# A context Fourier pipeline, shared bias buffers, spread row operations and a fifth begun pair in a two-layer hybrid kernel

## Chip, cores and metric

The kernel runs on one core of a Trainium2 chip. The metric is the device time of one execution in microseconds (us), median of several runs. The engines are named as the profile names them: PE (TensorE, matrix products), DVE (VectorE), ACT (ScalarE), POOL (GpSimd) and SP (SyncE, which issues most loads).

## What is computed

Two layers over 1024 latent tokens and 256 context tokens, width 1024. Layer 0 mixes tokens by a Fourier transform over half of the channels and a two-step long convolution over the other half; layer 1 is a neighbourhood attention with a bias. Each layer ends in a gated FFN, and each mixer and FFN is modulated by six vectors per layer.

```python
for i in range(DEPTH):                       # DEPTH = 2
    sh1, sc1, g1, sh2, sc2, g2 = ada_mod(c, ada_w[i], ada_b[i])      # silu(c) @ w + b, six parts
    u_lat = modulate(rms_norm(h_lat, norm1_g[i]), sh1, sc1)
    ...
    if even: y_lat = mixer_ab(u_lat, *ab); y_ctx = mixer_ab(u_ctx, *ab)
    else:    y_lat, y_ctx = mixer_na(u_lat, u_ctx, w_qkv, w_out, rpb, not last)
    h_lat = h_lat + g1 * y_lat
    h_lat = h_lat + g2 * swiglu(modulate(rms_norm(h_lat, norm2_g[i]), sh2, sc2), gate, up, down)
    ...

def mixer_ab(u, ...):
    p = u @ w_in                              # 1024 -> 2048
    y_f = fourier_mix(p[..., :512])           # 4 groups: real part of fft2 over (tokens, 128 channels)
    y_h = hyena_mix(p[..., 512:], ...)        # short_conv, then v = x1*long_conv(v); v = x2*long_conv(v)
    return concatenate([y_f, y_h]) @ w_out

# attention, per head and chunk of 16 columns: local scores + bias, context scores, one softmax over both
s_loc = q @ k_local * scale + bias;  s_ctx = q @ kc * scale
p = softmax(concatenate([s_loc, s_ctx]));  o = p_loc @ v_local + p_ctx @ vc
```

## The kernel before

All data stand transposed, channels on the 128 partitions, tokens along a row: pieces 0 and 1 are the two halves of the latent tokens (512 each), piece 2 is the context (256). Products are made in three passes, since every operand is split into a high part (cast by ACT, L326) and a low part (difference by DVE, L328): high by high, low by high, high by low. A PSUM tile is `ps` or `pq`, after the pool of banks it comes from. `s`, `t`, `tk`, `g`, `wh`, `wl`, `ws` are SBUF pools with a fixed number of buffers each, taken in turn; a load or a write into a buffer waits until the last reader of that buffer is done. A scheduler sets the order of each engine's instructions from the order in which the program makes them, and each engine runs its own in that order. Generators carry side work: the program calls `next` on one of them between blocks of the main work, and the side work of one step stands behind that block.

The stages that the change touches, with their time in the profiled execution:

- **Input projection** (205 to 470 us), `in_proj`: sixteen blocks of 128 output channels, 24 products on each piece (`lin`). After each block one step of each generator is made: filters of the context (`filt`), one column of the modulation vectors (`ada`, `ada_group`: a column is a 512 KB load and four DVE reductions with their row sum, L507), and from the seventh block on one step of `four`, which is `fourier_c`, the context's Fourier part: for each of four groups it loads the projected rows, folds them (POOL and ACT), multiplies by the channel matrices (`channels`, PE, then splits on ACT and DVE), multiplies by the token matrix (PE) and writes the result (`fourier_out`). One step is one group, with all of this in sequence. `conv` begins the context's convolution in the last two blocks. Modulation groups 2 and 3, eight columns each, are made here, group 4 in the output projection.
- **Convolution** (470 to 680 us): `forward_c` transposes the context's value and multiplies it with class matrices; `turned` (L981) transposes the latent value into eight tiles, each split by ACT and DVE; `unit` makes the two spectra of one frequency block and class, in two halves, and hands them to `combine_l` (L949), which multiplies with the filter on DVE and POOL; `turn_x` (L1006) transposes the gate. Eight units make order 0, then `inverse_first` goes back to tokens for the first gate, and eight more units make order 1: the first halves of four of these are begun in `inverse_first`. Matrices are loaded in float32 and cast by ACT (`cmat`, `cmat2`, L374 and L388), or loaded by POOL's queue with the cast in the transfer (`cast`), into the weight pools.
- **Output projection** (680 to 800 us), `out_proj`: group 0 is pieces 2 and 0, group 1 is piece 1. `fill` gives side work between blocks; here that is modulation group 4. `after1` is called behind each group: it normalises the context, then runs all steps of `wino_first`, the first sums of the FFN's Winograd form, behind group 0.
- **First FFN, context part** (800 to 930 us): `load_cond` (L488) loads the two condition vectors again and applies Silu on ACT.
- **Attention** (1750 to 2215 us), `attn_item`: 64 items (16 heads, two row halves, two pairs of column chunks). An item takes two 192 KB bias tiles from pool `G`, makes local and context scores on PE, adds the bias and takes the row maximum on DVE (L2091, `st` and `g`), exponentials on ACT, transposes on PE (L2108), splits them on ACT and DVE (L2111, L2112), and multiplies with the values.
- **Last FFN's start** (2275 to 2335 us): pairs of products are begun (`wino_begin`) before the normalisation's factor `r1` is known, since the factor can be applied to the product. `wino_second` then makes the sums that need the factor (T1 splits, L1495 on ACT and L1496 on DVE), which the product L1605 waits for.

## Time and profile before

| | |
|---|---|
| median of three runs | 2943.41 us (2942.9 to 2945.5) |
| profiled execution | 2940.22 us |
| its span, first to last instruction | 2938.5 us (1.7 us lie around it) |
| mean granted PE clock | 0.987 |
| PE busy in the span | 2824.0 us, 96% |
| DVE, ACT, POOL busy | 2044.7, 1334.5, 534.0 us |
| sum of PE's idle gaps ahead of products | 106.9 us |

A row of waits reads "engine, line and tile that waited <- engine, tile and line that released it: us in total, times, longest". A row by stretch reads "start:end length, then busy us (and count) of PE, PE's weight loads, DVE, ACT and POOL, then granted clock as a share of full speed, DMA share, GB/s". Busy time and waits overlap between engines; only what PE waits for lengthens a stage in which PE is last.

### The profile page before, as it was taken

How to read it: one execution, taken by the hardware profiler on the slowest of the kernel's cores; microseconds unless marked ns; L12 is line 12 of the kernel's file. 1: busy time of each engine (PE TensorE's matmuls, PEld its weight loads, DVE VectorE, ACT ScalarE, POOL GpSimd, SP SyncE). 2: the span in 40 equal slices, each digit the busy share in tenths (PEclk: the TensorE clock that was granted, in tenths of full speed). 3: DMA queues.
4: the chain of work that ended last, by engine and by line, in shares of the span. 5: the costliest groups of instructions: out<-in, count | busy, mean ns of one | idle time of the engine just before them, and what ended most of it. 6: DMA issues, size and time to landing. Idle time of an engine off the chain costs nothing.

```text
span 2938.5 us, 44126 instructions
## 1 busy us (share of the span) xinstructions
PE 2824.0 (96%) x15704; PEld 2361.3 (80%) x15704; DVE 2044.7 (70%) x3742; ACT 1334.5 (45%) x2282; POOL 534.0 (18%) x860
## 2 busy tenths in 40 slices
PE   8899998899999999999999999999989899999998
PEld 3678787788899888888888888888777688888886
DVE  6775676859776888966777536677668877765555
ACT  4543324543454333333445327777655533333433
POOL 2112112351100211212010002333212022111000
PEclk9999999999999999999999999999999999999999
DMA  9664434566556555659884446777846276434763
GB/s 338 218 214 157 150 103 130 186 220 230 201 175 194 196 199 199 226 183 331 303 309 153 138 130 153 179 194 174 238 144 239 80 243 218 169 110 163 229 194 129
DMA packets 303914, 568.39 MB, mean 193 GB/s; under 512 B 83144, under 2 KB 129930, under 8 KB 303694
## 3 DMA queue, kind: packets, MB, share of 16 engines
q1 hardware_dynamic: 242750, 373.11, 40.9%
q0 software_dynamic: 58640, 188.26, 18.1%
q10 hardware_dynamic: 2304, 4.20, 0.4%
q8 instruction: 124, 2.03, 0.3%
q14 instruction: 96, 0.79, 0.1%
HBM read 415.49 MB, written 119.80 MB: 182 GB/s over the span
## 4 chain that ended last, share of the span: by engine, by line
PE 73%; issue 10%; DMA 8%; DVE 5%; ACT 2%; POOL 1%; SPq 1%; POOLq 0%; DVEq 0%; ACTq 0%
PE ps L1605 24%; PE ps L322 23%; PE pq L322 12%; PE ps L1777 5%; PE pq L1605 3%; PE ps L1889 2%; PE pq L1777 2%; DMA s<-d 1%; DMA g<-in_bias 1%; PE ps L2108 1%; DMA mat<-in_ada_k 1%; DMA s<-in_c_ctx 1%; PE ps L1111 1%; DMA s<-in_x_t 1%; DVE wl L328 1%
## 5 line engine op out<-in xcount | busy, mean ns | idle before, releaser
L1605 PE MATMUL ps<-s,s 128*128 128x512 f32 x2008 | 498.2, 391 | 6.0 <-DVE s L1496 4.7
L1605 PEld LDWEIGHTS ps<-s,s 128*128 128x128 f32 x2008 | 377.4, 188 | 88.0 <-DVE s L1496 6.7
L322 PE MATMUL ps<-s,wh 128*128 128x256 f32 (+1 forms) x1584 | 356.4, 327 | 4.1 <-ACT wh L326 3.9
L322 PE MATMUL pq<-s,wh 128*128 128x512 f32 (+1 forms) x1040 | 319.7, 384 | 6.0 <-ACT s L794 2.1
L322 PEld LDWEIGHTS ps<-s,wh 128*128 128x128 f32 x1584 | 264.1, 191 | 29.9 <-ACT wh L326 5.2
L322 PE MATMUL ps<-s,s 128*128 128x65 f16 (+4 forms) x2780 | 241.2, 240 | 25.9 <-DVE st L2091 12.8
L1777 PE MATMUL ps<-s,s 128*128 128x512 f32 (+1 forms) x1000 | 259.5, 383 | 3.1 <-DVE s L328 3.0
L328 DVE TENSOR_TENSOR wl<-ws,wh 128x1024 fp32r<-128x1024 f32 (+1 forms) x142 | 169.7, 1196 | 127.0 <-ACT wh L326 122.5
L326 ACT CAST s<-s 128x1024 fp32r<-128x1024 f32 (+2 forms) x184 | 168.1, 941 | 190.3 <-DMA s<-d 161.4
L326 ACT CAST wh<-ws 128x1024 fp32r<-128x1024 f32 (+1 forms) x142 | 145.7, 1026 | 233.8 <-PE ps L322 90.2
L322 PE MATMUL ps<-s,wl 128*128 128x256 f32 (+1 forms) x792 | 237.5, 326 | 2.7 <-DVE wl L328 2.7
L322 PEld LDWEIGHTS pq<-s,wh 128*128 128x128 f32 x1040 | 192.2, 192 | 42.6 <-ACT s L794 3.4
L326 ACT CAST s<-t 128x512 fp32r<-128x512 f32 (+1 forms) x213 | 121.9, 587 | 220.2 <-PE ps L1605 81.9
L328 DVE TENSOR_TENSOR s<-s,s 128x1024 fp32r<-128x1024 f32 (+2 forms) x162 | 185.6, 1177 | 49.1 <-ACT s L326 46.6
L1777 PEld LDWEIGHTS ps<-s,s 128*128 128x128 f32 x1000 | 184.6, 188 | 40.9 <-DVE s L328 4.4
L322 PE MATMUL pq<-s,wl 128*128 128x512 f32 (+1 forms) x520 | 197.5, 381 | 1.5 <-DVE wl L328 1.5
L322 PE MATMUL ps<-s,mat 128*128 128x512 f32 x714 | 180.5, 403 | 18.6 <-ACT s L326 11.0
L328 DVE TENSOR_TENSOR s<-t,s 128x512 fp32r<-128x512 f32 (+1 forms) x213 | 138.1, 658 | 77.6 <-ACT s L326 49.4
L1605 PE MATMUL ps<-s,wh 128*128 128x512 f32 x608 | 189.0, 390 | 0.0
L322 PEld LDWEIGHTS ps<-s,mat 128*128 128x128 f32 x714 | 135.8, 193 | 55.3 <-ACT s L326 13.7
L322 PEld LDWEIGHTS ps<-s,wl 128*128 128x128 f32 x792 | 148.0, 190 | 15.9 <-DVE wl L328 3.5
L322 PEld LDWEIGHTS ps<-s,s 128*128 128x128 f32 (+1 forms) x860 | 132.7, 194 | 31.2 <-ACT s L326 9.9
(436 smaller groups left out, 5532.9 us busy)
## 6 DMA issues: line engine op xcount, KB each, us to landing
s<-d SPq DMA_DIRECT2D x283, 256.0 KB, 4.0
s<-in_down SPq DMA_DIRECT2D x150, 256.0 KB, 3.9
d<-s POOLq DMA_DIRECT2D x137, 256.0 KB, 3.1
s<-in_ada_w POOLq DMA_DIRECT2D x64, 512.0 KB, 5.1
d<-tk POOLq DMA_DIRECT2D x98, 256.0 KB, 3.5
g<-in_bias SPq DMA_DIRECT2D x128, 192.0 KB, 2.8
ws<-in_up SPq DMA_DIRECT2D x44, 512.0 KB, 4.0
d<-g POOLq DMA_DIRECT2D x87, 256.0 KB, 3.0
```

What stands on the lines that cost most here:

```text
L322: self.nc.tensor.matmul(o, l, r, start=st, stop=sp)
L326: self.last_hi = nc.scalar.copy(hi, src).ins
L328: self.last_lo = eng.tensor_tensor(lo, src, hi.bitcast(F32), SUB).ins
L1111: nc.tensor.matmul(d, s, w, start=cb not in first, stop=e == 1 and i == 1 and f == 3 and k == 2, skip_group_check=True)
L1605: nc.tensor.matmul(ps, x[:, sl], y, start=first and j == 0 and x is wh and y is xh, stop=j == 3 and x is wl, skip_group_check=True)
L1777: m = nc.tensor.matmul(acc[j][:, c0:c1], x[:, sl], y[:, xs], start=first and k == 0, stop=last and k == 2, skip_group_check=True)
L1889: m = nc.tensor.matmul(o, x[:, nb * P:(nb + 1) * P], t[:, c:c + 256], start=kb == 0 and k == 0 and nb % 2 == 0, stop=kb == NFB - 1 and k = ...
L2108: nc.tensor.transpose(ps[:, j * P:(j + 1) * P], src[:, j * P:(j + 1) * P], self.ident)
```

## The change

Seven edits. `fourier_c` becomes a pipeline of seven steps, begun one block earlier: in one step the output of group k−3, the token product of group k−2, the channel products of group k−1 and the fold of group k. Modulation group 4 moves from the output projection into the input projection, where two columns are made a step for eleven steps. The class matrices of the context are loaded by the casting queue, its class steps move from the projection's end into the first two units, and PE's gate transposes follow the last value transpose. Two of the second convolution's units get matrices by the casting queue in `S4` buffers (`cast4`), and the eighth takes banks of the other pool. `wino_first` becomes side work of the output projection's group 1, whose weights are fetched two ahead; the reload of the conditions ahead of that projection goes. `load_cond` moves from after the first FFN's context blocks into their last stage. Every second attention item (`c0` not 0) takes one 768-wide tile from the weight pool `ws` and one load instead of two. Before the last FFN a fifth half, (2, 0), is begun.

The diff, cut to its core:

```diff
@@ -398,2 +398,8 @@
 
+    def cast4(self, src):
+
+        m = self.S4(F32R)
+        self.ldr(m, src)
+        return m
+
     def lin(self, wh, wl, off, ks, x, pcs, view=lambda x: x):
@@ -841,6 +847,6 @@
                     next(g, None)
-            if i > 5:
+            if i > 4:
                 next(four, None)
-            if i > 13:
-                next(conv, None)
+            if i == 14:
+                next(conv)
             if nb < 4:
@@ -895,2 +901,6 @@
         PS = self.PS if o == 0 else self.PQ
+        if o == 0:
+            ms = [self.S2(F32R), self.S2(F32R)]
+            for i in range(4):
+                self.ldr(ms[i // 2][:, i % 2 * 256:i % 2 * 256 + 256], a["vf_c"][i, 0])
         for j in (0, 1):
@@ -907,3 +917,3 @@
                 xh, xl = tr[(i + i // 2) % 2]
-                mt = self.cmat(256, a["vf_c"][i, 0], small=o == 0)
+                mt = ms[i // 2][:, i % 2 * 256:i % 2 * 256 + 256] if o == 0 else self.cmat(256, a["vf_c"][i, 0])
                 ps = PS()
@@ -980,3 +990,4 @@
             for cb in range(4):
-                nc.tensor.transpose(ps[:, cb * P:(cb + 1) * P], self.ab["l"][cb][:, j * P:(j + 1) * P], self.ident)
+                last = nc.tensor.transpose(ps[:, cb * P:(cb + 1) * P], self.ab["l"][cb][:, j * P:(j + 1) * P], self.ident)
+            self.after_turned = last.ins
             hi, lo = self.S2(F32R), self.S2(F32R)
@@ -1005,3 +1016,4 @@
             x = (self.xrev if rev else self.xrow)[cb][:, j * P:j * P + P]
-            self.nc.tensor.transpose(ps[:, cb * P:(cb + 1) * P], x, self.ident)
+            with self.follow(self.after_turned):
+                self.nc.tensor.transpose(ps[:, cb * P:(cb + 1) * P], x, self.ident)
         t = self.S2()
@@ -1010,3 +1022,3 @@
 
-    def unit(self, o, fb, cls, bank=None):
+    def unit(self, o, fb, cls, bank=None, wide=False):
 
@@ -1016,3 +1028,3 @@
             src = a["vfe_l"][fb]
-            mt = self.cast(1024, src) if o + fb == 0 else self.cmat(1024, src)
+            mt = self.cast4(src) if wide else self.cast(1024, src) if o + fb == 0 else self.cmat(1024, src)
             mats = [mt[:, :512], mt[:, 512:]]
@@ -1022,3 +1034,4 @@
             src = a["vfo_l"][fb]
-            mats = [self.cast(1024, src[:, j * 1024:j * 1024 + 1024]) for j in (0, 1)] if o + fb == 0 else self.cmat2(src)
+            half = [src[:, j * 1024:j * 1024 + 1024] for j in (0, 1)]
+            mats = [self.cast4(x) for x in half] if wide else [self.cast(1024, x) for x in half] if o + fb == 0 else self.cmat2(src)
             xs = [range(4, 8), range(4)]
@@ -1371,20 +1384,27 @@
             mats[i] = m
-        raws = []
-        for g in range(4):
-            p0, p1 = self.S2(F32, 128), self.S2(F32, 128)
-            self.ld(p0, self.pd[g][:, 0:128])
-            self.ld(p1, self.pd[g][:, 128:256])
-            prs = self.folded(p0, p1, P, q[:, g:g + 1], qn[:, g:g + 1], nc.gpsimd)
...
-            raw = self.S2()
-            self.fourier_out(ps[:, 0:128], ps[:, 128:256], raw, P, self.T)
-            raws.append(raw)
+        raws, prs, opd, got = [], {}, {}, {}
+        for k in range(7):
+            if k >= 3:
+                raw = self.S2(F32, 256)
+                ps = got.pop(k - 3)
+                self.fourier_out(ps[:, 0:128], ps[:, 128:256], raw, P, self.T)
+                raws.append(raw)
+            if 0 <= k - 2 < 4:
+                ae, ao, am = opd.pop(k - 2)
+                ps = got[k - 2] = self.PS()
+                for i, (xh, xl) in enumerate((ae, am, ao)):
+                    m = mats[i]
+                    self.mm(ps[:, :256], xh, m[:, :256], i == 0, False)
+                    self.mm(ps[:, :256], xl, m[:, :256], False, False)
+                    self.mm(ps[:, :256], xh, m[:, 256:], False, i == 2)
+            if 0 <= k - 1 < 4:
+                opd[k - 1] = self.channels(prs.pop(k - 1), cg, 1, self.PS)
+            if k < 4:
+                p0, p1 = self.S2(F32, 128), self.S2(F32, 128)
+                self.ld(p0, self.pd[k][:, 0:128])
+                self.ld(p1, self.pd[k][:, 128:256])
+                prs[k] = self.folded(p0, p1, P, q[:, k:k + 1], qn[:, k:k + 1], nc.gpsimd)
             yield
         self.middle(cgf, q, qn, mid, self.PS)
+        yield
         for g in range(4):
@@ -1416,2 +1436,3 @@
         fetch()
+        fetch()
         for g, pcs in enumerate(groups):
@@ -1444,4 +1465,2 @@
                                 evict(nb, pc, accs[(nb, pc)])
-                    if k:
-                        next(fill, None)
             for nb in range(0 if g else 4, KB):
@@ -1452,5 +1471,5 @@
                     evict(nb, pc, acc[pc])
-                if g == 0:
-                    next(fill, None)
-                    next(fill, None)
+                if g:
+                    with self.follow(self.last_lo):
+                        next(fill, None)
             after(pcs)
@@ -1690,3 +1709,2 @@
                 last = lo
-            self.load_cond()
             todo = (x for l1, m in [(0, 5)] + [(1, m) for m in range(6)]
@@ -1747,2 +1765,4 @@
                     sums(k)
+            if i == 0 and u is not None:
+                self.load_cond()
             for _ in range(3 if i < 8 else 2):
@@ -2066,9 +2086,14 @@
         rlo = 4 * hf
-        bias, loc = [], []
+        loc = []
         pctx = self.PS()
+        if c0:
+            t = self.W("ws", "bias", F32, 768)
+            self.ld(t.rearrange("p (i k) -> p i k", i=2), a["bias"][head, hf, c0:c0 + 2].rearrange("i p k -> p i k"))
+            bias = [t[:, :384], t[:, 384:]]
+        else:
+            bias = [self.G(F32, 384), self.G(F32, 384)]
+            for i in (0, 1):
+                self.ld(bias[i], a["bias"][head, hf, c0 + i])
         for i in (0, 1):
             c = c0 + i
-            b = self.G(F32, 384)
-            self.ld(b, a["bias"][head, hf, c])
-            bias.append(b)
             q = [t[:, c * P:(c + 1) * P] for t in qs]
@@ -2270,3 +2295,3 @@
         self.load_cond()
-        ada = (x for m in (2, 3) for x in self.ada_group(0, m, (0, 1), "s2"))
+        ada = (x for m in (2, 3, 4) for x in self.ada_group(0, m, (0, 1), "s2"))
         filt = (x for g in (self.filter_raw("c", raws["c"]), self.filter_spectrum("c", 0, raws["c"][0]),
@@ -2290,3 +2315,3 @@
         fc, cc = four(), conv()
-        self.in_proj(u, ((filt, (1,)), (ada, (1,))), fc, cc)
+        self.in_proj(u, ((filt, (1,)), (ada, (2,) * 11 + (1, 1, 1, 0))), fc, cc)
         drain(ada)
@@ -2297,3 +2322,2 @@
         self.banks = 6
-        next(cc, None)
         self.xt, self.sums_due = {}, None
@@ -2307,6 +2331,6 @@
             self.turn_x(k)
-            if k == 6:
+            if k in (0, 1, 6):
                 next(cc)
         self.parts()
-        units = [self.unit(1, fb, cls, self.PQ if k == 3 else None)
+        units = [self.unit(1, fb, cls, self.PQ if k % 4 == 3 else None, k in (2, 3))
                  for k, (fb, cls) in enumerate(((0, 1), (1, 1), (2, 1), (0, 0), (1, 0), (3, 1), (2, 0), (3, 0)))]
@@ -2355,10 +2379,14 @@
                 load_h((1,))
-                for _ in self.wino_first(h, 0, 3, rs[1]):
-                    pass
+                rest.append(rs[1])
             else:
+                drain(first)
                 rest.append(self.rms((1,))[0])
 
+        def first_row():
+            yield from self.wino_first(h, 0, 3, rest.pop())
+
+        first = first_row()
+
         load_h((2, 0))
-        self.load_cond()
-        self.out_proj("w_out", y, [(2, 0), (1,)], h, 0, 2, after1, self.ada_group(0, 4, (0, 1), "s4"))
+        self.out_proj("w_out", y, [(2, 0), (1,)], h, 0, 2, after1, first)
         for b in range(8):
@@ -2493,2 +2521,3 @@
         begun[(1, 1)] = self.wino_begin(1, 1, 1, self.TK, self.S2)
+        begun[(2, 0)] = self.wino_begin(1, 2, 0, self.G, self.S2)
         self.ffn(1, None, h4, hs1, self.wino_second(h2, 1, 3, r1), after4, begun=begun)
```

Where instructions now stand. First PE at the end of the input projection; `pq` and `ps` are the last block's sums, `s_..` the operands, `g` the gate's rows. Before:

```order
L322 MATMUL ps_1128_4377<-s2_1106_4248,s2_1127_4374 128x512
L322 MATMUL ps_1128_4377<-s2_1107_4249,s2_1127_4374 128x512
L322 MATMUL ps_1128_4377<-s2_1106_4248,s2_1127_4374 128x512
L322 MATMUL ps_1131_4385<-s2_1109_4257,s2_1130_4382 128x512
L322 MATMUL ps_1131_4385<-s2_1110_4258,s2_1130_4382 128x512
L322 MATMUL ps_1131_4385<-s2_1109_4257,s2_1130_4382 128x512
L1006 MATMUL pq_1199_4594<-c_1_86,g_1193_4580 128x128
L1006 MATMUL pq_1199_4594<-c_1_86,g_1195_4584 128x128
```

After:

```order
L322 MATMUL ps_1174_4423<-s4_502_1610,wl_1172_4418 128x512
L322 MATMUL ps_1175_4424<-s4_503_1611,wl_1172_4418 128x512
L991 MATMUL ps_1179_4514<-c_1_86,s4_1097_3909 128x128
L991 MATMUL ps_1179_4514<-c_1_86,s4_1118_4036 128x128
L991 MATMUL ps_1179_4514<-c_1_86,s4_1137_4160 128x128
L991 MATMUL ps_1179_4514<-c_1_86,s4_1150_4283 128x128
L991 MATMUL ps_1182_4523<-c_1_86,s4_1097_3909 128x128
```

Before, the context's class products (two groups of three) and the gate's transposes (L1006) follow the last block, and the value's transposes (L981) come later; now the value's transposes (L991) follow at once, all eight tiles of them, and the gate's transposes come behind these.

Second PE at the last FFN's start. L1605 before and L1624 after are products of the FFN; those on `wh` and `wl` are begun pairs, those on two `s` tiles are the first product that needs the T1 splits. Before:

```order
L1605 MATMUL ps_5083_24195<-s2_5005_23847,wh_5079_24175 128x512
L1605 MATMUL ps_5083_24195<-s2_5004_23846,wl_5080_24176 128x512
L1605 MATMUL ps_5368_24452<-s4_5330_24338,s2_5024_23926 128x512 x2
L1605 MATMUL ps_5368_24452<-s4_5330_24338,s2_5025_23927 128x512
L1605 MATMUL ps_5368_24452<-s4_5331_24343,s2_5024_23926 128x512 x2
L1605 MATMUL ps_5368_24452<-s4_5331_24343,s2_5025_23927 128x512
L1605 MATMUL ps_5368_24452<-s4_5332_24348,s2_5024_23926 128x512 x2
L1605 MATMUL ps_5368_24452<-s4_5332_24348,s2_5025_23927 128x512
```

After:

```order
L1624 MATMUL ps_5053_24143<-s4_4937_23641,wh_5051_24138 128x512 x2
L1624 MATMUL ps_5055_24158<-s4_4940_23657,wh_5051_24138 128x512 x2
L1624 MATMUL ps_5340_24415<-s4_5302_24301,s2_4990_23854 128x512 x2
L1624 MATMUL ps_5340_24415<-s4_5302_24301,s2_4991_23855 128x512
L1624 MATMUL ps_5340_24415<-s4_5303_24306,s2_4990_23854 128x512 x2
L1624 MATMUL ps_5340_24415<-s4_5303_24306,s2_4991_23855 128x512
L1624 MATMUL ps_5340_24415<-s4_5304_24311,s2_4990_23854 128x512
L1624 MATMUL ps_5053_24143<-s4_4937_23641,wl_5052_24139 128x512
L1624 MATMUL ps_5053_24143<-s4_4946_23679,wh_5051_24138 128x512 x2
L1624 MATMUL ps_5053_24143<-s4_4946_23679,wl_5052_24139 128x512
```

Before, the T1 product follows the last begun pair; now it starts inside a begun pair, the fifth, (2, 0) (`ps_5053`, `ps_5055`), whose remaining products stand between the third and the fourth T1 operand.

Third ACT at the end of the first FFN's context part. L488 before and L494 after are Silu on the reloaded conditions, L326 casts of weights. Before:

```order
L1684 ACTIVATE t_2330_9070<-ps_2328_9020 128x256
L488 ACTIVATE s4_2366_9288<-s4_2366_9288 128x512 x2
L326 CAST wh_2348_9155<-s4_2347_9154 128x1024
L1684 ACTIVATE t_2341_9140<-ps_2339_9090 128x256
L326 CAST wh_2356_9219<-s4_2355_9218 128x1024
L1684 ACTIVATE t_2352_9210<-ps_2350_9160 128x256
L488 ACTIVATE s4_2367_9293<-s4_2367_9293 128x512 x2
L326 CAST wh_2359_9225<-s4_2358_9224 128x1024
```

After:

```order
L1703 ACTIVATE t_2328_9062<-ps_2326_9012 128x256
L494 ACTIVATE s4_2417_9540<-s4_2417_9540 128x512
L326 CAST wh_2346_9147<-s4_2345_9146 128x1024
L1703 ACTIVATE t_2339_9132<-ps_2337_9082 128x256
L494 ACTIVATE s4_2417_9540<-s4_2417_9540 128x512
L494 ACTIVATE s4_2418_9545<-s4_2418_9545 128x512
L326 CAST wh_2354_9211<-s4_2353_9210 128x1024
L1703 ACTIVATE t_2350_9202<-ps_2348_9152 128x256
L326 CAST wh_2357_9217<-s4_2356_9216 128x1024
L494 ACTIVATE s4_2418_9545<-s4_2418_9545 128x512
```

The call moved in the code, but the four activations still stand among the casts of the same weights; the pairs are apart now.

More of the change, by code (lines that the diff above doesn't have):

```diff
@@ L1371, in fourier_c @@
             mats[i] = m
-        raws = []
-        for g in range(4):
-            p0, p1 = self.S2(F32, 128), self.S2(F32, 128)
-            self.ld(p0, self.pd[g][:, 0:128])
-            self.ld(p1, self.pd[g][:, 128:256])
-            prs = self.folded(p0, p1, P, q[:, g:g + 1], qn[:, g:g + 1], nc.gpsimd)
-            ae, ao, am = self.channels(prs, cg, 1, self.PS)
-            ps = self.PS()
-            for i, (xh, xl) in enumerate((ae, am, ao)):
-                m = mats[i]
-                self.mm(ps[:, :256], xh, m[:, :256], i == 0, False)
-                self.mm(ps[:, :256], xl, m[:, :256], False, False)
-                self.mm(ps[:, :256], xh, m[:, 256:], False, i == 2)
-            raw = self.S2()
-            self.fourier_out(ps[:, 0:128], ps[:, 128:256], raw, P, self.T)
-            raws.append(raw)
+        raws, prs, opd, got = [], {}, {}, {}
[20 more added lines that the diff above has]
+                prs[k] = self.folded(p0, p1, P, q[:, k:k + 1], qn[:, k:k + 1], nc.gpsimd)
             yield
         self.middle(cgf, q, qn, mid, self.PS)
+        yield
         for g in range(4):
```

## The prediction

> **What bounds the kernel now.** I read the page's busy times first, then who waited for whom on TensorE (PE), then busy time and granted clock by stage. Page:
>
> ```profile
> PE 2824.0 (96%) x15704; PEld 2361.3 (80%) x15704; DVE 2044.7 (70%) x3742; ACT 1334.5 (45%) x2282; POOL 534.0 (18%) x860
> ```
>
> PE is busy 2824 us of a span of 2938.5, so it bounds the kernel. The diff takes no matrix product away; a change that only moves work can therefore win PE's idle 114 us, and what slow clock follows that idle time. Who ends the idle time (line waited for: us in total, times, longest):
>
> ```profile
> PE ps L322 <- ACT s L326: 18.1, 12, 5.2
> PE ps L322 <- DVE st L2091: 12.8, 8, 3.1
> PE pq L1006 <- DVE s L816: 6.1, 1, 6.1
> PE ps L1605 <- DVE s L1496: 4.7, 3, 2.9
> PE ps L322 <- DVE s L949: 4.6, 1, 4.6
> ...
> PE ps L322 <- ACT mat L388: 1.7, 1, 1.7
> ```
>
> Where it lies, one stage a row (stretch, its length, busy us of PE, PEld, DVE, ACT, POOL with counts, granted clock, DMA share, GB/s):
>
> ```profile
> 205.00:320.00 115.00, 112.51 (x609) 96.14 (x609) 69.85 (x180) 37.32 (x80) 24.95 (x38) 0.99 0.43 145
> 320.00:400.00 80.00, 72.97 (x390) 61.21 (x389) 49.96 (x163) 25.75 (x60) 4.80 (x5) 0.96 0.38 127
> 400.00:470.00 70.00, 70.00 (x356) 59.29 (x355) 53.07 (x124) 14.90 (x22) 17.12 (x19) 1.00 0.35 113
> 470.00:490.00 20.00, 11.60 (x57) 9.35 (x56) 15.24 (x25) 10.38 (x19) 5.02 (x4) 0.83 0.27 92
> 566.00:615.00 49.00, 38.26 (x157) 30.15 (x155) 33.30 (x39) 19.15 (x21) 17.17 (x11) 0.93 0.66 225
> 680.00:800.00 120.00, 116.59 (x613) 98.95 (x611) 98.38 (x209) 49.62 (x81) 16.77 (x32) 1.00 0.61 223
> 905.00:930.00 25.00, 22.08 (x177) 21.68 (x176) 11.15 (x14) 10.60 (x17) 3.26 (x6) 0.95 0.69 219
> 1780.00:2215.00 435.00, 407.07 (x3829) 355.37 (x3827) 298.23 (x684) 314.40 (x709) 119.08 (x190) 0.98 0.72 184
> 2300.00:2335.00 35.00, 28.98 (x112) 21.30 (x111) 35.00 (x57) 19.11 (x34) 0.00 (x0) 0.90 0.09 30
> 2400.00:2500.00 100.00, 100.00 (x443) 82.81 (x442) 72.75 (x110) 33.58 (x55) 21.67 (x40) 1.00 0.61 213
> ```
>
> The first seven are the input projection (three rows), its end, the second convolution's spectra, the output projection and the end of the first FFN's context part; then attention and the last FFN's start. The last row is the rate without waits: 443 matrix products in 100 us, 0.226 us each. After many waits the clock is halved for a while:
>
> ```profile
> 326.90:330.30 3.40, 3.39 (x14) 3.15 (x15) 1.29 (x5) 1.65 (x6) 0.00 (x0) 0.50 0.02 5
> 477.10:483.90 6.80, 5.38 (x20) 4.73 (x21) 6.11 (x13) 2.03 (x5) 0.59 (x1) 0.50 0.50 174
> 576.10:579.50 3.40, 3.06 (x8) 2.15 (x7) 3.40 (x7) 1.84 (x3) 0.00 (x0) 0.50 1.01 375
> 610.20:613.60 3.40, 3.40 (x10) 2.66 (x9) 3.40 (x4) 0.00 (x0) 2.70 (x2) 0.50 0.13 51
> 2125.70:2129.10 3.40, 3.40 (x15) 2.72 (x12) 2.46 (x7) 1.75 (x5) 0.52 (x1) 0.50 0.82 241
> 2183.70:2190.50 6.80, 5.58 (x42) 5.10 (x42) 5.23 (x12) 2.70 (x7) 0.00 (x0) 0.50 0.12 45
> 2306.60:2313.40 6.80, 4.49 (x9) 2.65 (x10) 6.80 (x12) 3.41 (x6) 0.00 (x0) 0.50 0.00 0
> ```
>
> I count half of PE's busy time in such a stretch as lost: 1.7 us for a short one, 2.7, 2.8 and 2.2 us for the three long ones. These losses go if the wait ahead of them goes.
>
> The wait ahead of the stretch at 2125.7 is no long one:
>
> ```profile
> 2124.84 1.12 PE L322 MATMUL ps<-s,s 128*128 128x65 f16 x30 [2.38 <-DVE st L2091]
> ```
>
> 2.38 us of idle time were enough. The Trainium skill ("TensorE: Matmul & The Clock Gate", section on the HAM clock gate) says that the half clock sets in after at least one idle window of about 3.4 us. By that rule waits shorter than 3.4 us would earn no clock back, and of the credits below the 4.5 us for attention and the 2 for the FFN would fall; here the row differs, so the measurement decides and I keep them.
>
> **The change, part by part.** For each part: the most it can win (idle plus half-clock loss), what it adds, and the value I take.
>
> *A, input projection (205 to 470).* The context's Fourier part ran fold, channel products, group product and output of one group in one step, serially; now each of seven steps holds one stage of up to four different groups, so PE meets operands made a projection block earlier. PE's idle time from 320 to 400 is 80 − 73.0 = 7.0 us; the half-clock stretch at 327 is 1.7. Against it stands modulation group 4 (eight columns), which moves here from the output projection, two columns a step instead of one. What the eight cost there, on DVE alone and in line L507 alone:
>
> ```profile
> 690.00:745.00 55.00, 20.92 (x64) 1.00 0.55 203
> ```
>
> So 21 us of DVE work and eight 512 KB loads on SP join stretches where DVE now works 69.9 + 50.0 = 120 us of 195: on average 141 of 195, still beside PE. But DVE takes instructions in order, and it stands behind those loads (205 to 400):
>
> ```profile
> DVE tk L507 <- DMA s<-in_ada_w: 18.9, 4, 8.4
> ...
> DVE t L507 <- DMA s<-in_ada_w: 4.5, 4, 2.8
> ```
>
> A wait there holds up the low parts of the next weights (L328), which PE needs. Upper end 8.7; lower end by the rival below. I take +2: half of that less some 2 us of new waits.
>
> *B, end of the projection (470 to 490).* Now PE goes from the last block to the context's class products and the gate's transposes (L1006), whose bank is freed by the short convolution's L816 (6.1 us), then to the transposes of the value (L981). Afterwards it goes straight to the eight value transposes, whose inputs are made blocks earlier; the class products move among the first units. Idle 20 − 11.6 = 8.4, clock 2.7: at most 11.1. What remains: eight transposed tiles wait for banks which ACT and DVE free by splitting,
>
> ```profile
> L328 DVE TENSOR_TENSOR s<-t,s 128x512 fp32r<-128x512 f32 (+1 forms) x213 | 138.1, 658 | 77.6 <-ACT s L326 49.4
> ```
> ```profile
> 604.23 1.03 PE L899 MATMUL pq<-c,s 128*128 128x128 f32 x8
> ```
>
> 8 × 0.66 = 5.3 us of splits on DVE beside 32 transposes, four times the second row, 4.1 us: a stall of at least 1.2, and the short convolution's own row operations come first on DVE. I put the stall at 5 in all (as long as the splits) and take +6; bounds 0 to 11.
>
> *C, second convolution (566 to 615).* Two units get matrices by a casting DMA into buffers of their own, so their first halves can stand before PE's wait: 42 instead of 24 products in front of it, 18 × 0.226 = 4.1 us more cover. Who ended PE's idle time in this stretch:
>
> ```profile
> PE ps L322 <- ACT s L326: 4.2, 2, 3.9
> ```
>
> The cover hides that 3.9 us wait and the change drops the ACT cast wait (1.7, L388) and the stretch at 576 (1.5). The fourth unit of each four takes the other bank pool, which is against the 4.6 us wait on L949 and its stretch at 610 (1.7); yet L949 must still come in DVE's order, so I take none of it. +7; bounds 0 and 49 − 38.3 + 3.2 = 13.9.
>
> *D, output projection.* Idle 120 − 116.6 = 3.4 there; the 21 us leave DVE, weights are fetched one further ahead, and the first Winograd sums move from one block after group 0 into the blocks of group 1. +2; bounds −3 (these sums now late) to +3.4.
>
> *E, reload of the conditions.* In the code it moves behind the first block's row; in ACT's order the four activations stay between the casts of the same weights, and these casts wait behind them now:
>
> ```profile
> ACT s L488 <- DMA s<-in_c: 5.8, 2, 4.7
> ...
> ACT s L488 <- DMA s<-in_c_ctx: 4.3, 2, 3.4
> ```
>
> Idle 25 − 22.1 = 2.9 stays: 0, bounds −1 to +2.9.
>
> *F, attention.* Every second item takes its two bias tiles as one 384 KB load into the four-deep weight pool; the others keep both G buffers, so loads can be asked for about four items ahead instead of two. 128 loads become 96. Now:
>
> ```profile
> DVE g L2091 <- DMA g<-in_bias: 19.3, 14, 3.1
> ...
> DVE s L2112 <- ACT s L2111: 41.5, 22, 3.9
> ```
>
> The first row is the wait that should vanish; behind it on DVE stand the row maximum and all that follows, and PE waits for L2091 12.8 us (8 times). The clock lost at 2125.7 and 2183.7 is 1.7 + 2.8 = 4.5. At most 17.3. DVE then waits for ACT as in the second row, so I take not half: +8. Weights share the pool, but a weight load is asked for some 600 products before its use, at 435/3829 us a product about 70 us. Lower end −2.
>
> A page bears on the joining of loads: the Trainium skill ("DMA: Bandwidth & Descriptors", section Bandwidth) advises batches of 1 MiB and more, since each transfer carries a fixed cost. By that rule the joined load alone would earn something; here the present 192 KB loads land in 2.8 us (median), no run shows a joined one, and I count nothing for it.
>
> ```profile
> g<-in_bias SPq DMA_DIRECT2D x128, 192.0 KB, 2.8
> ```
>
> *G, last FFN's start.* A fifth half (24 products, 24 × 0.226 = 5.4 us) is begun ahead, and the normalisation's end stands one begun pair earlier, so the T1 splits (L1496) start up to 5.4 us sooner and have 5.4 more to hide behind, against 4.7 us of waits. Idle 35 − 29 = 6.0 and clock 2.2: at most 8.2. DVE is full in that stretch (35.0 of 35), so the fifth pair's own splits (about 3 us) come off: +5; bounds −1 to 8.2.
>
> **Sum.** 2 + 6 + 7 + 2 + 0 + 8 + 5 = 30 us. The profiled execution took 2940.22 us (span 2938.5 and 1.7 around it): 2910. The runs' median is 2943.4, 3.2 above, so 2913 is my forecast, 1.0% faster.
>
> **The rivals.** (1) *The waits only change names.* In C, F and G the releaser is DVE, and DVE's own queue (L2112 behind ACT, L949, full at 2300) is then the limit; left are A 2, B 6, the 3.9 + 1.5 of C and D 2, less 3 of new DVE waits: 12, so 2931. For it: 41.5 us of DVE waits that no edit touches; against: in attention DVE is busy 298 of 435. Chance 0.20. (2) *Everything acts.* 9 + 11 + 14 + 3 + 0 + 13 + 8 = 58, the upper bounds with attention at three quarters, and I leave 3 of it for new waits: 55, so 2888. Chance 0.10. (3) *An edit does nothing*: the moved condition reload, by the order of ACT. It is in my sum at 0; if it did act, 2.9 less. (4) *Slower: DVE becomes the bound in the input projection.* In order, each step now stands behind two modulation loads. DVE's free time from 205 to 470 is 265 − 173 = 92 us, 71 after the moved work, so 5.9 us for each of the twelve double steps. If the second load comes later than that, each us more costs 12. At the longest wait seen, 8.4, it is 2.5 × 12 = 30 and twelve short half-clock stretches, 20: 50 against the 28 of B to G, 22 slower: 2965. For it: four such waits already, 4.7 us on average; against: that is below 5.9, and the second row of part A has none above 2.8. Chance 0.13. (5) *Halfway to that*, gains and loss cancel, 2943: 0.07.
>
> **How the numbers follow.** Forecast 0.50 (2913, 2898 to 2925), rivals as above. Range 2888 to 2946: from everything acting to a cancelled gain, leaving out rival 4 and a little below. About 0.2% (6 us) is what a measurement can tell from no change: faster 0.50 + 0.20 + 0.10 = 0.80, same 0.07, slower 0.13.
>
> **What would show it.** After: no wait of PE on L816's successor, PE below 3 us idle at 470 to 490; no DVE wait for bias loads, and the PE row for the bias line under 6 us; no wait over 1 us for T1 splits; the casts of two units gone from ACT; the row of modulation waits on DVE under 25 us. I am wrong if PE is idle over 15 us between 205 and 470, or if attention stays near 435 us with DVE waiting for ACT in place of the loads.

## The result, and the profile after

The changed kernel takes 2925.23 us (median of 4 runs, 2923.48 to 2929.05) against 2943.15 before: ratio 0.994, 95% interval 0.9923 to 0.9958, about 18 us less. The forecast was 2913, so direction and range hold and the gain is 18 us where 30 stood in the sum. The profiled span is 2921.6 us against 2938.5. The page's busy times:

```profile
PE 2821.2 (97%) x15704; PEld 2361.3 (81%) x15704; DVE 2045.4 (70%) x3742; ACT 1325.3 (45%) x2271; POOL 533.0 (18%) x859
```

As many products as before; only waiting and slow clock changed. By stretch, cut in both traces at the same products (the last of the projection's blocks, the last value transpose L981 or L991, the inverse's first and last product, the FFN's first, the first and the last attention transpose, the 801st product of the last FFN):

| stretch | before | after | forecast gain | gain |
|---|---|---|---|---|
| input projection (A) | 263.4 | 266.2 | 2 | −2.8 |
| its end, to the last value transpose (B) | 18.5 | 7.7 | 6 | 10.8, or 7.2 without the moved products |
| spectra and units, then the inverse's end (C) | 125.1 + 69.1 | 124.9 + 74.3 | 7 | −5.0, or −1.4 without them |
| output projection to FFN (D, E) | 248.4 | 247.6 | 2 | 0.8 |
| attention (F) | 431.5 | 417.0 | 8 | 14.5 |
| last FFN's start (G) | 257.6 | 258.3 | 5 | −0.7 |

Twelve class products (12 × 0.226 = 2.7 us) and eight gate transposes (8 × 0.11 = 0.9 us) moved from B's stretch to C's. The other stretches lie within 1.1 us. The changed kernel's rows by stretch (the two parts of C are rows 3 and 4; columns as before):

```profile
207.20:473.40 266.20, 255.71 (x1353) 218.77 (x1352) 193.03 (x550) 76.59 (x159) 49.05 (x65) 0.97 0.44 145
473.40:481.10 7.70, 5.37 (x35) 5.16 (x34) 7.12 (x14) 6.82 (x12) 0.00 (x0) 0.78 0.55 175
481.10:606.00 124.90, 114.57 (x525) 92.99 (x523) 94.37 (x123) 61.45 (x81) 54.51 (x45) 0.97 0.59 197
606.00:680.30 74.30, 70.38 (x466) 65.13 (x467) 46.83 (x88) 31.76 (x55) 28.94 (x35) 0.93 0.62 203
1777.80:2194.80 417.00, 400.66 (x3818) 351.96 (x3816) 297.76 (x682) 309.32 (x702) 119.25 (x190) 0.99 0.73 192
2194.80:2453.10 258.30, 248.46 (x1109) 201.14 (x1108) 211.59 (x323) 116.09 (x193) 46.43 (x86) 0.99 0.56 195
```

In attention DVE has no wait for bias loads left (it had 19.3 us), and its wait for ACT's L2136 is a little longer. The list of DVE's waits there begins:

```profile
DVE s L2137 <- ACT s L2136: 47.1, 25, 3.9
DVE st L2158 <- PE ps L322: 17.6, 16, 2.9
```

PE's waits over the whole span (of the changed kernel; L2116 is the bias line, L959 the combination, L515 the row sum of a modulation column, L539 the sum of squares):

```profile
PE ps L322 <- ACT s L326: 9.9, 6, 5.2
PE ps L322 <- DVE s L328: 6.6, 5, 4.0
...
PE ps L322 <- DVE st L2116: 3.8, 4, 1.1
PE pq L322 <- DVE c L515: 3.6, 1, 3.6
PE pq L322 <- DVE s L959: 3.4, 1, 3.4
PE ps L322 <- DVE tk L539: 3.2, 1, 3.2
```

Of the old heads of the list, the wait for L816 is gone and those for T1 splits are smaller; the wait for the combination is not: L949 is L959 now, and 4.6 us have become 3.4 beside further waits of 2.0 and 2.3. The last three rows are one single wait each, and each lies in a stretch that lost.

### The profile page after: what moved, and what is told of

Same layout as the page of the kernel before. It is cut to its first block, busy times and chain, and to the rows that moved or that the text cites. A ratio compares the mean times of both kernels' runs of the same rounds, so it can differ in the third digit from the quotient of the medians.

```text
span 2921.6 us, 44070 instructions
## 1 busy us (share of the span) xinstructions
PE 2821.2 (97%) x15704; PEld 2361.3 (81%) x15704; DVE 2045.4 (70%) x3742; ACT 1325.3 (45%) x2271; POOL 533.0 (18%) x859
## 5 line engine op out<-in xcount | busy, mean ns | idle before, releaser
L1624 PE MATMUL ps<-s,s 128*128 128x512 f32 x1956 | 483.6, 389 | 0.3 <-ACT s L326 0.3
L1624 PEld LDWEIGHTS ps<-s,s 128*128 128x128 f32 x1956 | 367.0, 188 | 77.6 <-ACT s L326 1.1
L322 PE MATMUL ps<-s,wh 128*128 128x256 f32 (+1 forms) x1700 | 386.0, 333 | 8.6 <-DVE s L328 4.6
L322 PEld LDWEIGHTS ps<-s,wh 128*128 128x128 f32 x1700 | 284.8, 193 | 39.7 <-DVE s L328 5.5
L322 PE MATMUL pq<-s,wh 128*128 128x512 f32 (+1 forms) x924 | 278.9, 378 | 3.4 <-DVE s L2429 2.0
L328 DVE TENSOR_TENSOR wl<-ws,wh 128x1024 fp32r<-128x1024 f32 (+1 forms) x141 | 168.7, 1197 | 143.8 <-ACT wh L326 139.3
L326 ACT CAST wh<-ws 128x1024 fp32r<-128x1024 f32 (+1 forms) x141 | 144.7, 1026 | 262.2 <-PE ps L322 129.9
L1797 PE MATMUL ps<-s,s 128*128 128x512 f32 (+1 forms) x1000 | 259.8, 383 | 3.3 <-DVE s L328 3.1
L322 PE MATMUL ps<-s,wl 128*128 128x256 f32 (+1 forms) x850 | 254.5, 331 | 0.5 <-DVE wl L328 0.5
L326 ACT CAST s<-s 128x1024 fp32r<-128x1024 f32 (+2 forms) x184 | 167.8, 940 | 191.2 <-DMA s<-d 166.7
L328 DVE TENSOR_TENSOR s<-s,s 128x1024 fp32r<-128x1024 f32 (+2 forms) x162 | 185.5, 1176 | 56.5 <-ACT s L326 54.0
L1797 PEld LDWEIGHTS ps<-s,s 128*128 128x128 f32 x1000 | 184.4, 188 | 41.7 <-DVE s L328 5.4
L326 ACT CAST s<-t 128x512 fp32r<-128x512 f32 (+1 forms) x208 | 119.9, 590 | 177.6 <-PE ps L1624 73.3
L322 PEld LDWEIGHTS pq<-s,wh 128*128 128x128 f32 x924 | 168.3, 190 | 33.5 <-DVE s L2429 2.4
L1624 PE MATMUL ps<-s,wh 128*128 128x512 f32 x600 | 187.4, 392 | 0.0
L328 DVE TENSOR_TENSOR s<-t,s 128x512 fp32r<-128x512 f32 (+1 forms) x208 | 136.7, 667 | 67.4 <-ACT s L326 44.4
L322 PE MATMUL ps<-s,mat 128*128 128x512 f32 x678 | 171.5, 399 | 11.3 <-ACT s L326 6.9
L322 PE MATMUL pq<-s,wl 128*128 128x512 f32 (+1 forms) x462 | 173.3, 377 | 0.0
L322 PEld LDWEIGHTS ps<-s,wl 128*128 128x128 f32 x850 | 159.1, 192 | 16.5 <-DVE wl L328 0.8
```

Of the source, the lines that this page charges most:

```text
L322: self.nc.tensor.matmul(o, l, r, start=st, stop=sp)
L326: self.last_hi = nc.scalar.copy(hi, src).ins
L328: self.last_lo = eng.tensor_tensor(lo, src, hi.bitcast(F32), SUB).ins
L1624: nc.tensor.matmul(ps, x[:, sl], y, start=first and j == 0 and x is wh and y is xh, stop=j == 3 and x is wl, skip_group_check=True)
L1797: m = nc.tensor.matmul(acc[j][:, c0:c1], x[:, sl], y[:, xs], start=first and k == 0, stop=last and k == 2, skip_group_check=True)
```

## Experiments

The theory after the result: the bias edit carries the whole gain; in the projection the pipeline wins and the second modulation column a step loses; among the units a bank choice loses what the casting queue wins; at the last FFN the fifth half moves idle time. The main rival: the new waits are noise of one trace, or come from something ahead of them.

**Bias edit alone.** The kernel before with only:

```diff
...
+        if c0:
+            t = self.W("ws", "bias", F32, 768)
+            self.ld(t.rearrange("p (i k) -> p i k", i=2), a["bias"][head, hf, c0:c0 + 2]...)
...
```

> The kernel before with the attention bias edit alone. If the 14.6 us that the changed kernel won between the first and the last transpose of attention (431.3 to 416.7 us) are this edit's, attention takes 416 to 419 us here and the kernel is 13 to 16 us faster than before (about 2928 us). If part of that came from what runs ahead of attention (another order of loads, another state of the buffers), attention gains under 8 us.

2926.74 us, ratio 0.9946 (0.9933 to 0.996); attention:

```profile
1777.60:2192.10 414.50, 398.48 (x3818) 348.83 (x3816) 297.55 (x682) 309.08 (x702) 119.36 (x190) 1.00 0.73 193
```

17.0 us less than before, and all other stretches within 3 us of before. In all thirteen kernels here that have this edit attention takes 414.5 to 418.2 us, against 431.5 before. So this edit alone gives what the whole change gives, and all the others together come to about nothing.

**Lead or joined load.** The changed kernel with

```diff
-            self.ld(t.rearrange(...), a["bias"][head, hf, c0:c0 + 2]...)
+            for i in (0, 1):
+                self.ld(bias[i], a["bias"][head, hf, c0 + i])
```

> The changed kernel, each wide bias tile filled by two 192 KB loads instead of one of 384 KB. If the gain is the longer lead of the loads (more buffers), nothing is lost: attention stays at 416 to 418 us and no wait of DVE for bias loads comes back. If the gain is the joined load (fewer transfers), up to half of the 14.6 us is lost: attention at 420 to 425 us.

2921.36 us (ratio 0.993, 0.9918 to 0.9942); attention 417.0 us, to the tenth as with the joined load, and no wait for bias loads. The gain is the lead: buffers, not the number of transfers.

**Group 4 back**, with one column a step, and **serial Fourier part** with two:

```diff
-        ada = (x for m in (2, 3, 4) for x in self.ada_group(0, m, (0, 1), "s2"))
+        ada = (x for m in (2, 3) for x in self.ada_group(0, m, (0, 1), "s2"))
-        self.in_proj(u, ((filt, (1,)), (ada, (2,) * 11 + (1, 1, 1, 0))), fc, cc)
+        self.in_proj(u, ((filt, (1,)), (ada, (1,))), fc, cc)
...
```

> The changed kernel with modulation group 4 back in the output projection, one column a step in the input projection; the pipeline of the context's Fourier part stays. If the second column a step, with DVE in order behind its load, costs what the pipeline wins, the 4.0 and 3.6 us waits at 320 and 359 go and the input projection takes 258 to 261 us from its first block to its last product, against 263.5 before and 266.3 in the changed kernel; the output projection pays 1 to 3 us, so the kernel is 2 to 6 us faster than the changed one. If the pipeline itself slows the projection, it stays at 264 us or more.

> The changed kernel with the serial Fourier part of before, two columns a step kept. If the pipeline wins some 5 us and the columns cost some 8, the projection takes 270 to 275 us here, 4 to 8 more than in the changed kernel. If the pipeline wins nothing, it stays at 265 to 268 us.

The first: 2916.25 us, ratio 0.991 (0.9896 to 0.9923). The second: 2936.39 us, 0.9973 (0.9963 to 0.9984). The projection in each:

```profile
208.80:459.70 250.90, 249.81 (x1353) 214.66 (x1352) 172.48 (x465) 75.84 (x159) 48.42 (x65) 0.99 0.42 137
```
```profile
205.40:479.80 274.40, 257.54 (x1353) 219.67 (x1352) 192.63 (x550) 77.66 (x159) 47.35 (x65) 0.96 0.43 141
```

With before and after that makes four corners: serial and one column 263.4, pipeline and one column 250.9, pipeline and two 266.2, serial and two 274.4. The pipeline wins 12.5 with one column and 8.2 with two; the second column costs 15.3 with the pipeline. The first run was better than its expectation (258 to 261): PE is idle only 1.1 us in it. Its output projection and the FFN's context part (D and E) pay more than the 1 to 3 us expected: 255.5 us against 247.6.

**Why the columns cost so much: loads or DVE's work?** Two runs. One asks for each column's load a column earlier; the other lets every second column work on data that are already there (twelve loads left out).

```diff
+                st = getattr(self, "ada_next", None) or two(m * 8)
+                self.ada_next = two(nb + 1) if nb + 1 < last else None
```
```diff
+                if nb % 2:
+                    st = self.cond[0]
+                else:
```

> The changed kernel with each modulation column's load asked for one column earlier (one more pair of buffers in use); the same DVE work, two columns a step. The columns cost 13.7 us of projection beside the pipeline (459.7 against 473.4 at its last product). If most of it is DVE standing behind loads (22.9 us of waits there now), these waits fall under 8 us and the projection ends at 462 to 467. If it is DVE's work and order, the waits fall but the end stays at 470 to 475.

> The changed kernel in which every second modulation column of the input projection works on the condition vectors, already on the chip, instead of its own weights: twelve of the 24 loads of 512 KB are left out, DVE's reductions stay (so the modulation vectors of these columns are not the reference's). Seven runs with two loaded columns a step end the projection at 469 to 480 us; with one column a step it ended at 459.7. If the loads are the cost (DVE waits behind them, and they stand on SP behind stores that wait for DVE), the end comes to 459 to 464 us and the DVE waits for these loads fall to about 18 us or less. If DVE's work is the cost (18 us more of L513 in this stretch), it stays at 468 us or later.

2919.67 us (0.991, 0.9882 to 0.9939) and 2925.91 us (0.9946, 0.9928 to 0.9965). Asking earlier did not bring the data in time: DVE still waits 21.6 us for them (24.7 in the changed kernel), and the projection ends at 469.3, between the two expectations. It takes 260.7 us, 5.5 less than in the changed kernel, so a small gain is not excluded. What SP does in the changed kernel's projection points to the reason; its queue, which carries these loads, waits for DVE itself (L822 is the short convolution, whose result SP stores):

```profile
SPq L307 <- DVE wl L328: 68.0, 5, 27.5
SPq L307 <- DVE s L822: 61.8, 8, 14.3
```

Without half of the loads:

```profile
206.90:469.60 262.70, 253.35 (x1353) 216.75 (x1352) 191.97 (x550) 75.60 (x159) 48.98 (x65) 0.98 0.38 123
```

3.5 us less than after, of 15.3; six kernels with the changed kernel's projection code spread from 262.4 to 268.5, so even that is not certain. DVE's waits for loads (19.4 us) are here about what they are with one column a step (18.3 us), yet PE is idle 9.4 us here and 1.1 there, and the end, 469.6, is the second reading's. What differs is DVE's work (192 us of 263 against 172 of 251): most of the cost is that work and where it stands, not the loads. The loads have a part in it. In the changed kernel the first of PE's two long waits in this stretch follows one of DVE's, on a load:

```profile
324.44 0.80 PE L322 MATMUL ps<-s,wh 128*128 128x256 f32 x2 [4.04 <-DVE s L328]
```
```profile
323.48 0.69 DVE L513 CUSTOM_DVE_ANT_0 t<-s,s 128x512 f32<-128x512 f32 x1 [5.40 <-DMA s<-in_ada_w]
```

The second shows how work costs PE time on an engine that is free for a quarter of the stretch. PE, then a few of DVE's rows in the changed kernel:

```profile
358.14 1.24 PE L322 MATMUL ps<-s,s 128*128 128x256 f32 x9
363.00 0.56 PE L322 MATMUL pq<-c,t 128*128 128x1 f32 x2 [3.62 <-DVE c L515]
```
```profile
358.65 0.69 DVE L513 CUSTOM_DVE_ANT_0 t<-s,s 128x512 f32<-128x512 f32 x1
...
359.95 1.22 DVE L328 TENSOR_TENSOR wl<-ws,wh 128x1024 fp32r<-128x1024 f32 x1
361.09 0.68 DVE L513 CUSTOM_DVE_ANT_0 t<-s,s 128x512 f32<-128x512 f32 x1
...
362.65 0.21 DVE L1316 TENSOR_TENSOR s<-pq,t 128x64 f32<-128x64 f32 x1
362.78 0.14 DVE L515 TENSOR_TENSOR c<-ah 128x1 f32<-128x1 f32 x1
```

From 358.65 DVE works without a gap, weight split and column reductions mixed, until it comes to what PE waits for. The profile names L515, but the waiting product is a sum over a filter (`filter_sum`), which reads no modulation column. More likely it waits for its bank: L1316, the last row of a Fourier output, reads a `pq` tile just before, and in the run without half of the loads the profile names that line (there L1319) at the same product.

**The units.** The bank rule alone back, then all of the units' edit back:

```diff
-        units = [self.unit(1, fb, cls, self.PQ if k % 4 == 3 else None, k in (2, 3))
+        units = [self.unit(1, fb, cls, self.PQ if k == 3 else None, k in (2, 3))
```
```diff
+        units = [self.unit(1, fb, cls, self.PQ if k == 3 else None)
```

> The changed kernel, the eighth unit of the second order back on the first bank pool; the two units with matrices by the casting queue stay. The changed kernel takes 124.9 and 74.3 us from the last value transpose to the inverse's first product and to its last, 199.2 in all, against 125.1 and 69.1 before. If the new 3.4 us wait for the other pool's bank is what the eighth unit's bank choice brings, the sum falls by 3 to 5 us. If DVE's combining work sets the pace whichever bank is used, the wait comes back under the first pool's name and the sum stays within 1 us.

> The changed kernel with the second order's units as before: old banks and all matrices cast by ACT. If the casting queue's early halves gain the 7 us forecast and something else loses them, the two stages take 203 us or more here. If the edit of the units is itself what makes the inverse late, they take 194 to 197 us. If neither matters (DVE's combining sets the pace), 198 to 200.

2921.65 us (0.9918, 0.9895 to 0.9941) and 2924.79 us (0.9933, 0.9911 to 0.9955). The two parts of C, first with the bank rule back, then with all back:

```profile
476.10:602.40 126.30, 116.64 (x533) 94.73 (x531) 98.68 (x127) 62.13 (x82) 55.43 (x45) 0.97 0.62 206
602.40:671.00 68.60, 66.25 (x459) 60.78 (x458) 42.59 (x86) 32.21 (x57) 29.11 (x35) 1.00 0.62 205
```
```profile
482.60:612.30 129.70, 117.62 (x534) 96.12 (x532) 98.16 (x125) 64.37 (x85) 55.59 (x43) 0.95 0.58 192
612.30:680.70 68.40, 66.75 (x465) 61.12 (x464) 43.72 (x86) 32.33 (x57) 28.47 (x34) 1.00 0.63 209
```

194.9 us, 198.1 us, and 199.2 after; the eight kernels here that share the changed kernel's units took 197.5 to 201.2. So the matrices by the casting queue win 3.2 us. That is no more than this spread, but two waits can be named for it: PE waits 3.9 us for ACT's L326 and 1.7 for its L388 with all back, and for neither with the bank rule back alone. The eighth unit in the other pool loses 4.3, and the inverse shows it: 74.3 us after, 68.6 with the bank rule back. The expectation's other reading holds too, in part: the wait for L959 does come back under the first pool's name,

```profile
PE ps L322 <- DVE s L959: 5.3, 2, 2.9
```

but the inverse behind it is short again.

**The last FFN.** The factor's sums written one half later, and the fifth half left out:

```diff
+        begun[(0, 1)] = self.wino_begin(1, 0, 1, self.TK)
         c = self.rms_begin(1)
-        begun[(0, 1)] = self.wino_begin(1, 0, 1, self.TK)
+        begun[(1, 0)] = self.wino_begin(1, 1, 0, self.G, self.TK)
         r1 = self.rms_end(1, c)
...
-        begun[(1, 0)] = self.wino_begin(1, 1, 0, self.G, self.TK)
```
```diff
-        begun[(2, 0)] = self.wino_begin(1, 2, 0, self.G, self.S2)
```

> The changed kernel with the last FFN's normalisation sums one begun half later and its end behind the third half, written so in the program. In the changed kernel PE waits 3.2 us at 2264 for these sums, since they stand behind the first begun pair there. If that early place eats the fifth half's gain, the wait goes and the stretch from the last attention transpose to the 801st product of the last FFN falls from 258.3 us to 254 to 256, the T1 waits staying under 3 us. If the factor then comes too late, the T1 waits come back (4 to 7 us) and the stretch stays at 257 to 260.

> The changed kernel without the fifth begun half. From the last attention transpose to the 801st product of the last FFN it takes 258.3 us with it, 257.6 before. If the fifth half hides T1 waits as forecast, they come back here (3 to 5 us more) and the stretch is 261 to 264. If the half only moves idle time to later places (1.9 us at 2340 behind its own eviction, L1629), the stretch stays at 256 to 260 without that wait.

2918.22 us (0.9911, 0.989 to 0.9932) and 2921.37 us (0.9924, 0.9897 to 0.995). PE's waits from the last attention transpose on, of the changed kernel, of the later factor and of the kernel without the fifth half (L1515 is the T1 split, L1629 the copy of a begun product):

```profile
PE ps L322 <- DVE tk L539: 3.2, 1, 3.2
PE pq L1624 <- DVE s L1515: 2.0, 3, 0.9
PE pq L1624 <- ACT tk L1629: 1.9, 1, 1.9
```
```profile
PE ps L1624 <- DVE s L1515: 3.4, 2, 2.3
...
PE pq L1624 <- ACT tk L1629: 1.9, 1, 1.9
PE pq L1624 <- DVE s L1515: 1.2, 2, 0.6
```
```profile
PE ps L322 <- DVE tk L539: 3.2, 1, 3.2
PE ps L1624 <- DVE s L1515: 2.3, 1, 2.3
...
PE pq L1624 <- DVE s L1515: 1.5, 3, 0.7
```

The stretch takes 258.3, 260.6 and 262.7 us. Later, the factor's own wait goes and the T1 waits come back (4.6 us): nothing won. Without the fifth half they are 3.8 us, against 2.0 with it, so the half hides 1.8 us of them; with it stands a wait of 1.9 at 2340 for the copy of a begun product. That the stretch is 4.4 us longer without the half does not show what the half is worth: six kernels with the changed kernel's code and order of products here take 258.3 to 263.4 us, and PE's idle time in the stretch, 10.3 us without the half and 9.8 with it, is nearly the same. Nor do the medians rank these two kernels: their projections, with the same code, differ from the changed kernel's by up to 2 us.

The early sums are not the FFN's doing alone. In both runs of the units, and in the two below, the convolution's eighth unit stands on the first bank pool; there the scheduler puts these sums later, 1600 us behind the unit, and PE does not wait for them. In the three of them that have the fifth half the stretch takes 258.6 to 264.8 us, so that order wins nothing either.

**Only the parts that won**, and the same without the fifth half. Group 4 and the first Winograd sums as before, one column a step, the eighth unit on the first pool.

> The changed kernel with what the runs show as losses undone: modulation group 4 and the first Winograd sums back in the output projection as before, one column a step, the eighth unit on the first bank pool. By the stages measured apart: projection 251 (against 266), spectra and inverse 195 (against 199), output projection 248, the rest as in the changed kernel: 18 to 21 us faster than the changed kernel, about 2905. If the parts depend on one another (a wait removed shows the next), half of it: about 2915.

> The run with only the winning parts, and without the fifth begun half. If that half is worth something when the factor stands late, as it does there, this is 2 to 5 us slower than with it; if it only moves idle time, within 1 us.

2911.52 us, ratio 0.9885 (0.9864 to 0.9905), and 2913.24 us, 0.9898 (0.988 to 0.9917). The first lies between its two expectations and beats both kernels, 14 us under the changed one's median; its stretches A, C (both parts together) and D with E:

```profile
206.70:457.40 250.70, 248.81 (x1353) 213.67 (x1352) 172.46 (x465) 75.69 (x159) 48.77 (x65) 1.00 0.42 137
464.90:657.80 192.90, 182.80 (x990) 155.92 (x990) 140.50 (x210) 93.10 (x137) 84.77 (x80) 0.97 0.62 205
657.80:912.00 254.20, 242.01 (x1659) 221.45 (x1658) 188.43 (x321) 118.50 (x178) 29.45 (x55) 0.98 0.60 202
```

Projection and units came out as measured apart; the output projection did not (254.2, not 248), though group 4 and the first Winograd sums are made as before: PE waits 3.7 us at 692 for a weight's low part there, as it does in the run with group 4 back and did not before. The trace shows DVE at work without a gap from 678.3 us on, mostly on the group's column reductions, and that low part (L328) only at 694.7, 5.8 us after ACT's cast for it: the same queue in front of PE as in the projection. Why DVE came to it in time before stays open; it was not tried. The fifth half is worth 1.7 us by the medians here, which is less than the intervals, and 1.2 by the stretch (258.6 against 259.8).

## Why the prediction was right, and where its sizes were off

- **What bounds the kernel** and that nothing but idle time could be won: right; PE's busy time is 2821 us against 2824.
- **F** (+8): mechanism right, size too small. The step that failed is "DVE then waits for ACT, so I take not half": the wait for ACT grew only from 41.5 to 47.1 us, and 14.5 of the at most 17.3 came. PE's waits for the bias line are 6.6 us in all, against 14.7 before. The joined load counts for nothing, as taken (417.0 us both ways). The Trainium skill ("DMA: Bandwidth & Descriptors", section Bandwidth) advises larger transfers; no gain from them shows here, where the longer lead has left DVE no wait for these loads to shorten.
- **B** (+6): right, 7.2. PE is idle 2.3 us of 7.7, as the signal said; it is one wait, behind the short convolution's L824, where I put the stall at 5.
- **A** (+2): wrong, −2.8 (from +1.0 to −5.1 in the six kernels with this code). The step that failed is "on average still beside PE", with 2 us for new waits: the pipeline wins 12.5, more than its upper end of 8.7, of which I took half, and the columns cost 15.3. The fourth rival had the place and the direction but only the smaller part of the cause: it priced the loads (twelve double steps, where the edit makes eleven), and most of it is DVE's work ahead of what PE needs. DVE's waits for loads reached 24.7 us, against 23.6 before.
- **C** (+7): wrong, −1.4. The casting queue won 3.2, of 7.1 forecast; the step that failed is the bank choice, which I counted at nothing and which lost 4.3. That is the first rival, the waits change names, in one stretch.
- **D, E** (+2, 0): 0.8 together. A new wait of 2.3 us for a normalisation's sums (L539, at 798) stands against what D won. The wait behind the condition reload stayed, as the order had it, and grew (2.2 to 3.7 us).
- **G** (+5): −0.7 (to −5.8 in the six kernels with this code and order). The T1 waits fell from 4.7 to 2.0 as forecast; the step that failed is that the early end of the normalisation costs nothing. PE reached its sums 3.2 us before they were there. Where another edit put the sums later, nothing was won either, and that part stays open.
- **The clock.** I credited short waits too. The changed kernel's row at 473 bears that out: one wait of 2.3 us, and a granted clock of 0.78. The Trainium skill ("TensorE: Matmul & The Clock Gate", section on the HAM clock gate) asks for a whole idle window of about 3.4 us, so the measurement decides again. The new waits bring lost clock with them: the inverse's row stands at 0.93, at 1.00 before.

The sum was nearer than its terms: F and B gave 8 us more than taken, A, C and G 19 less. That they cancel in part is luck.

## What to carry to other kernels

Spreading a serial side task over steps can be worth much (12.5 us here), but only while the engine that serves it in order has room at the places where the main engine waits, not on average. More buffers ahead of a load can be worth all the rest of a change; test such an edit alone. And a choice of bank or order at one place is a wait at another: read the row behind the removed wait before crediting it.

## What was not expected of the hardware

Waits of a few us at the same product, in identical code, differ between traces: the projection took 262.4 to 268.5 us in six kernels that share the changed kernel's code for it and run its products in the same order. So a stretch cut at the same products shows where time went, but a difference of 3 us between two single traces says little unless a wait that comes or goes can be named beside it.
